# An encoder layer on one core: first MLP product with banks seeded by ScalarE, weight sums on VectorE, functions a step later

## The chip, the cores and the metric

The kernel runs on one core of one Trainium2 chip. The metric is the device time of one execution in microseconds (us). The core has TensorE (PE; PEld is its weight load), VectorE (DVE), ScalarE (ACT), GpSimd (POOL) and SyncE (SP), which here issues nearly all DMAs. A matmul writes to PSUM, eight banks of 128 x 512 fp32; everything else works from SBUF.

## What is computed

One layer of an encoder on 2048 tokens of width 1024: a mixer (two kinds of attention), and then the MLP, which is what matters here:

```python
x = x + gt1 * (mixed @ w_o)
h = rmsnorm(x, g_norm2) * (1.0 + sc2) + sh2
x = x + gt2 * (jnp.square(jax.nn.relu(h @ w1)) @ w2)
```

Here `w1` is 1024 x 4096 and `w2` 4096 x 1024. All values are fp32.

## The kernel before

**Precision.** Each fp32 operand is held as two parts: the high part is ScalarE's cast to fp32r, the low part is VectorE's subtraction of that from the fp32 value (`split`, `operand`). A product takes three matmuls: high x high, high x low, low x high, in this order (`mm3`).

**Seven products for eight.** Both MLP products work on 2 x 2 blocks with seven block products (1 to 7), some of whose operands are sums or differences of blocks. Token blocks of 512 (`tb`) come in two pairs, `mb` 1 (tokens 1024 to 2047) and `mb` 0. For the first product (class `First`, line 1431) a pair `j` of hidden tiles, 2 x 128 rows, takes seven *steps*, one for each block product; a step is 4 blocks of the contraction x 3 = 12 matmuls of 128 x 512. There are 16 pairs, so 112 steps for each `mb`.

- `sums` (1463) makes the four sums of weight tiles of a pair, on GpSimd, as soon as `fetch` is called, nine steps ahead of the pair (1839 to 1840); `load` (13 steps ahead) issues the two DMAs of 512 KB. For the very first pair `fetch` is called in the sixth row of the out-projection (`Mixed`, 1778, by `then`, 1821), for the second pair only when its first operand is prepared.
- The products of a pair run in the order `PRODUCTS` = 1, 6, 5, 7, 2, 3, 4 (1283). Products 1, 6, 5, 7 and 3 take a PSUM bank each; 2 adds onto the bank of 1, 4 onto that of 7. `run` (1475) ends with the reads of the bank: ScalarE copies product 1 to a tile `u`; VectorE adds 6 to it, makes `v` (5 + u), the hidden block c22 (7 + v), c12 (3 + v) and c21 (bank 7 + u); ScalarE makes c11 from bank 1.
- `hidden` (1521) puts relu and square of each block on ScalarE at once, behind the add; `keep` (1528) stores rows for later, and the differences of hidden blocks that the second product needs are made two ticks later (`rest`, `end`).

**Order.** All matmuls and, in this part, all instructions of every queue stand in the order in which the code issues them. The loop at the end of the kernel goes step by step: `prepare` of operands for the steps ahead (eight tiles of the pool `opp`: seven steps ahead in First, three in Second), then the jobs that `at(n, ...)` put at this step, then `run`, then a tick of `later`, a list of jobs that wait a number of ticks. So on every engine an instruction waits for all that stand ahead of it in its queue, and `later.add(1, ...)` means the end of the same step.

**Around it.** Ahead of First of `mb` 1 run the last eight rows of the out-projection (`Mixed`); each row ends in a VectorE add from its bank, and its store to DRAM two ticks later. Among these rows the right-hand operands of `mb` 1 are made by `right_blocks` (1369): load of four rows, a VectorE multiply with the norm's row and a ScalarE shift for each, and then in three jobs (`scale`, `mixed`, `rest`) the high and low parts of seven blocks. During First of `mb` 1, `norm2` (1337) makes the norm rows of token blocks 1 and 0: squares on ScalarE, sums on VectorE, column sums on TensorE (`pvm`), a root in five small GpSimd operations, a diagonal on VectorE (`ndgm`), and a matmul that spreads it (`psr`). VectorE also makes four sums a pair for the second product (`second_sums`, 1531, tiles `w2s`; for `mb` 0 `outer_sums`). Next comes `Second` of `mb` 1 (four products of 16 steps, four banks each), among which `right_blocks` makes the operands of `mb` 0, and `update` (1615) adds results to rows `scr_x`. Then First of `mb` 0, Second for products 1 and 6, and three `Outer` blocks, each a set of seven products on two column blocks, with Second of products 5 and 7 between them.

**Banks.** Four PSUM banks are `zb`, two are `db`, and two are `ab` (the accumulator pair of the attention). `pp` (1301) hands them out in turn, `zb, zb, ab, db, ...`, to all of these. `Outer` already seeds: when product 1 ends, ScalarE copies its bank to a second one, onto which 6, 7 and 4 add; 3 adds onto the bank of 5, and 2 onto that of 1 (`HOME`, 1286).

**Names in the profile.** Every instruction has line 42, the helper that keeps the order, so groups go by tiles: `ps<-h,opw` are the matmuls of First, `ps<-oph,opv` those of Second, `ps<-opr,ol` and `ps_s` those of Outer, `pso` those of the out-projection; `opr<-w` and `opw<-w` or `opw<-ts` are the parts of First's weights (`w` raw, `ts` sums), `cu`, `cv`, `cx`, `cy` the tiles u, v, c22 and c11, `ca`, `cb`, `ce` the differences, `cxr` and `xr` rows of the out-projection, `ty`/`cy` with `h` the right blocks, `txn` the norm's rows, `txu`/`txo` rows of results.

Of the kernel before, what the change touches and what calls it, by code (L numbers as in the profile page):

```python
# [79 lines left out]
def encoder_kernel(ctx, tc, xT, c, g1, g2, w_in, w_rest, gqk, bias, w_o, w1, w2, w_ada, b_ada, out):  # L80
# [1202 lines left out]
    PRODUCTS = (1, 6, 5, 7, 2, 3, 4)  # L1283
# [10 lines left out]
    if True:  # L1294
# [6 lines left out]
        pp = Banks(zb, zb, ab, db, zb, zb, ab, db)  # L1301

# [23 lines left out]
        def bank(nm):  # L1326
            return pp.tile([P, TB], F32, tag="ps", name=f"ps{nm}")
# [9 lines left out]
        def norm2(tb, step):  # L1337
# [14 lines left out]
            def second():  # L1352
                dg = norm_rstd(np2, pp, acc, f"m{tb}")

                def third():
                    pr = bank(f"r{tb}")
# [10 lines left out]
            at(step + 3 * KT + 4, lambda: later.add(2, second))  # L1367

        def right_blocks(mb, k, home):
# [20 lines left out]
            def scale():  # L1390
                for nm, tb, kk in tiles:
                    dve.tensor_tensor(y[nm], y[nm], rows[tb], op=ALU.mult)
                    act.activation(
                        y[nm], y[nm], AF.Identity, scale=aff[:, 1, kk : kk + 1], bias=mod[:, 3 * KT + kk : 3 * KT + kk + 1]
                    )
                high(1, "11")
# [22 lines left out]
            return load, scale, mixed, rest  # L1419
# [11 lines left out]
        class First(Step):  # L1431
# [4 lines left out]
            def __init__(self, mb, j, i):  # L1436
                self.mb, self.j, self.i, self.nm = mb, j, i, f"{mb}_{j}_{i}"
                if mb and j == 0 and i in PRODUCTS[:2]:
                    self.tiles = self.frees = 0

            def prepare(self, home=None):
                if (home is None) != (self.tiles > 0):
                    return
                d, j, i = self.fetch(), self.j, self.i
                src = {1: d["11"], 2: d["12"], 4: d["22"]}.get(i)
                self.w = operand(d["S", i] if src is None else src, f"w{self.nm}", dst=home)

            def load(self):
                d, j = First.pair.setdefault((self.mb, self.j), {}), self.j
                if not d:  # L1450
                    t = raw_pair([P, 2, KT, P], F32, f"w1_{self.mb}_{j}")
                    for s in range(2):
                        d[s] = t[:, s]
                        sp.dma_start(d[s], w1[2 * j + s])
                return d
# [7 lines left out]
            def sums(self, d):  # L1463
                for s in range(2):
                    d[f"{s + 1}1"] = d[s][:, 0:HK, :].rearrange("p k f -> p (k f)")
                    d[f"{s + 1}2"] = d[s][:, HK:KT, :].rearrange("p k f -> p (k f)")
                s1, s2, s4 = (temp(f"s{self.nm}_{n}") for n in (0, 1, 3))
                s3 = d["21"]
                column_sum(pool, s1, d["21"], d["22"], ALU.add)
                column_sum(pool, s2, s1, d["11"], ALU.subtract)  # L1470
                column_sum(pool, s3, d["11"], d["21"], ALU.subtract)
                column_sum(pool, s4, d["12"], s2, ALU.subtract)
                d["S", 5], d["S", 6], d["S", 7], d["S", 3] = s1, s2, s3, s4

            def run(self):
                d, i, nm = First.pair[self.mb, self.j], self.i, self.nm
                home = {2: 1, 4: 7}.get(i, i)
                if home == i:
                    d["ps", i] = bank(nm)
                ps = d["ps", home]  # L1480
                for k in range(HK):
                    ks = slice(k * P, (k + 1) * P)
                    h = hops[i, k]
                    first, last = home == i and k == 0, k == HK - 1
                    mm3(ps, self.w[:, 0, ks], self.w[:, 1, ks], h[:, 0, :], h[:, 1, :], first, last, home != i)
                if i == 1:
                    d["u"] = kept(f"u{nm}")
                    act.copy(d["u"], ps)
                if i == 6:
                    column_sum(dve, d["u"], ps, d["u"], ALU.add)  # L1490
                if i == 5:
                    d["v"] = column_sum(dve, kept(f"v{nm}"), ps, d["u"], ALU.add)
                if i == 7:
                    d["c22"] = self.hidden(column_sum(dve, kept(f"x{nm}"), ps, d["v"], ALU.add), 3)
                if i == 2:
                    d["c11"] = kept(f"y{nm}")
                    act.activation(d["c11"], ps, AF.Relu)
                    act.activation(d["c11"], d["c11"], AF.Square)
                    c11 = d["c11"]
                    later.add(2, lambda: self.keep(1, c11))  # L1500
                if i == 3:
                    c12 = self.hidden(column_sum(dve, d["v"], ps, d["v"], ALU.add))

                    def rest():
                        t1 = column_sum(dve, kept(f"a{nm}"), c12, d["c11"], ALU.subtract)
                        self.keep(5, t1)
                        d["t2"] = column_sum(dve, kept(f"b{nm}"), d["c22"], t1, ALU.subtract)
                        self.keep(6, d["t2"])
                        self.keep(7, column_sum(dve, c12, d["c22"], c12, ALU.subtract))

                    later.add(2, rest)
                if i == 4:
                    c21 = self.hidden(column_sum(dve, d["u"], ps, d["u"], ALU.add), 2)
# [5 lines left out]
                    later.add(2, end)  # L1519
# [95 lines left out]
        def update(mb, r, odd, acc, loads, adds, keep=True):  # L1615
# [354 lines left out]
```

## Time and profile before

| | |
|---|---|
| time, median of 3 runs (lowest to highest) | 2582.78 us (2579.35 to 2585.35) |
| the profiled execution: time, span | 2583.59 us, 2581.9 us |
| mean granted TensorE clock | 0.999 |
| PE busy in First of `mb` 1, Second of `mb` 1, First of `mb` 0, the rest | 311.85 of 320.07, 178.54 of 181.27, 306.21 of 306.91, 403.58 of 405.89 us |
| VectorE busy in the same stretches | 255.40, 136.78, 236.22, 337.86 us |
| waits of TensorE by engine, longest in total: `z` for VectorE `p` (attention) | 7.1 us in 15 |
| `psr` for VectorE `ndgm` | 4.9 us in 2 |
| `ps` for ScalarE `cu` | 2.4 us in 4 |

A row of a timeline gives the start and the length in us, the engine, the operation, output <- inputs, partitions x elements, the number of merged instructions, and in brackets the idle time ahead of it with the engine that ended it. A row of a stage table gives start:end, length, the busy us (and instructions) of PE, PEld, DVE, ACT and POOL, the granted TensorE clock, the DMA share and GB/s. PE's busy time is modelled, so an operand that comes a little late can lie inside it: a stage's length against its number of matmuls says more than its idle time.

### The profile page before, as it was taken

The numbers are of one execution on the slowest core, as the hardware profiler recorded it, in microseconds if no ns is written. First come the engines' busy times: TensorE is split into PE (matmuls) and PEld (weight loads), VectorE is DVE, ScalarE is ACT, GpSimd is POOL, SyncE is SP. The second block draws the span as 40 slices with busy tenths as digits, with TensorE's granted clock in tenths as the row PEclk, the third lists the DMA queues.
The fourth block names the chain that finished last, engine by engine and source line by source line (L and its number), as shares of the span: only waits on it lengthen the run. The fifth ranks groups of instructions, "written<-read, shape, count | busy, mean of one in ns | idle before, by whom it ended". The sixth has DMA issues, their size and how long they took to land. (4 is left out here: it accounts for less than half of the span.)

```text
span 2581.9 us, 39420 instructions
## 1 busy us (share of the span) xinstructions
PE 2546.8 (99%) x12484; PEld 2112.9 (82%) x12484; DVE 2031.6 (79%) x3401; ACT 1448.3 (56%) x2785; POOL 950.4 (37%) x1256
## 2 busy tenths in 40 slices
PE   9999999999999999999999999999999999999999
PEld 7888888888888888887888877887888878888887
DVE  7656767887789879998768787777787886798987
ACT  6333435668866676666744544565444445465655
POOL 4330144777766677677603333200123320000000
PEclk9999999999999999999999999999999999999999
DMA  9879879788887788756787876786577766866773
GB/s 354 330 296 363 336 286 290 215 238 277 272 262 233 234 281 260 240 195 195 226 331 245 290 261 247 261 302 236 212 248 266 250 241 241 315 222 242 266 272 123
DMA packets 276944, 674.80 MB, mean 261 GB/s; under 512 B 29952, under 2 KB 75008, under 8 KB 266112
## 3 DMA queue, kind: packets, MB, share of 16 engines
q1 hardware_dynamic: 275440, 667.57, 74.7%
q10 hardware_dynamic: 1296, 4.72, 0.4%
q8 instruction: 99, 1.62, 0.3%
q14 instruction: 109, 0.89, 0.1%
HBM read 461.93 MB, written 210.24 MB: 260 GB/s over the span
## 5 line engine op out<-in xcount | busy, mean ns | idle before, releaser
L42 PE MATMUL ps<-h,opw 128*128 128x512 f32 x2664 | 609.9, 390 | 4.0 <-ACT cu L42 2.4
L42 PEld LDWEIGHTS ps<-h,opw 128*128 128x128 f32 x2664 | 498.1, 188 | 113.8 <-ACT cu L42 5.7
L42 PE MATMUL ps<-oph,opv 128*128 128x512 f32 x1536 | 353.3, 391 | 2.7 <-ACT opv L42 1.6
L42 POOL TENSOR_TENSOR b<-p 128x512 f32<-128x512 f32 (+1 forms) x320 | 292.5, 914 | 168.1 <-DVE p L42 92.1
L42 ACT CAST wth<-wt 128x512 fp32r<-128x512 f32 (+3 forms) x544 | 257.7, 484 | 172.3 <-PE wt L42 162.3
L42 PEld LDWEIGHTS ps<-oph,opv 128*128 128x128 f32 x1536 | 289.0, 188 | 66.3 <-ACT opv L42 2.7
L42 DVE TENSOR_TENSOR wtl<-wt,wth 128x512 fp32r<-128x512 f32 (+3 forms) x544 | 291.7, 548 | 59.4 <-ACT wth L42 56.9
L42 PE MATMUL pt<-w,ht 128*128 128x512 f32 x1248 | 288.2, 391 | 0.0
L42 POOL TENSOR_TENSOR ts<-w 128x512 f32<-128x512 f32 x32 | 48.5, 1515 | 616.9 <-DMA w<-in_w_dram 516.0
L42 PEld LDWEIGHTS pt<-w,ht 128*128 128x128 f32 x1248 | 233.0, 188 | 47.7
L42 DVE TENSOR_TENSOR_SCAN p<-z,p,zero 128x512 f32<-128x512 f32 x192 | 245.9, 1282 | 25.7 <-ACT z L42 18.3
L42 PE MATMUL acc<-wth,v 128*128 128x512 f32 (+3 forms) x544 | 220.6, 410 | 0.0
L42 ACT ACTIVATE z<-z 128x512 f32<-128x512 f32 (+1 forms) x320 | 166.5, 521 | 55.1 <-PE z L42 49.3
L42 PE MATMUL z<-k,q 128*128 128x512 f32 (+3 forms) x640 | 185.6, 371 | 7.8 <-DVE p L42 7.1
L42 DVE TENSOR_TENSOR opw<-w,opw 128x512 fp32r<-128x512 f32 x127 | 100.8, 796 | 111.5 <-ACT opw L42 111.5
L42 PE MATMUL acc<-wtl,v 128*128 128x512 f32 (+3 forms) x544 | 185.4, 347 | 0.0
L42 POOL TENSOR_TENSOR e<-e,cols 128x640 f32<-128x640 f32 (+4 forms) x128 | 142.9, 1123 | 83.3 <-DVE cols L42 57.1
L42 PE MATMUL wt<-ident,b 128*128 128x128 f32 x1088 | 171.4, 273 | 1.0 <-DVE cols L42 0.3
L42 PEld LDWEIGHTS wt<-ident,b 128*128 128x128 f32 x1088 | 136.3, 140 | 42.2 <-DVE wtl L42 1.9
L42 PE MATMUL po<-fx,ow 128*128 128x512 f32 x576 | 161.7, 393 | 1.0 <-DMA ow<-scr_wo 1.0
L42 DVE TENSOR_TENSOR oph<-hw,oph 128x512 fp32r<-128x512 f32 x128 | 90.4, 706 | 80.0 <-ACT oph L42 80.0
L42 ACT CAST opr<-r 128x512 fp32r<-128x512 f32 x168 | 104.7, 625 | 83.2 <-PE ps L42 46.6
(210 smaller groups left out, 4849.2 us busy)
## 6 DMA issues: line engine op xcount, KB each, us to landing
q<-scr_q SPq DMA_DIRECT2D x128, 256.0 KB, 5.2
w<-in_w_dram SPq DMA_DIRECT2D x64, 512.0 KB, 5.5
hw<-scr_hid SPq DMA_DIRECT2D x64, 512.0 KB, 6.3
k<-scr_k SPq DMA_DIRECT2D x240, 128.0 KB, 4.4
v<-scr_v SPq DMA_DIRECT2D x120, 256.0 KB, 4.1
wa<-in_w_ada_dram SPq DMA_DIRECT2D x48, 512.0 KB, 6.2
ow<-scr_wo SPq DMA_DIRECT2D x24, 1024.0 KB, 5.9
hw<-scr_s SPq DMA_DIRECT2D x48, 512.0 KB, 7.0
```

The source lines that it names most:

```text
L42: return lambda *x, **y: self.tc.keep_in_program_order(f(*x, **y))
```

## The change

- First runs its products in the order 1, 5, 6, 3, 7, 2, 4 and uses the homes of `Outer`: product 1 ends in a ScalarE copy of its bank to another one, from the accumulator pair (`seeded`), onto which 6, 7 and 4 add; 3 adds onto the bank of 5. ScalarE copies products 5 and 6 out of their banks. VectorE makes only c12 (bank 5 + copy of 6) and c22 (bank 6 + copy of 5); ScalarE's relu reads c11 and c21 from the banks. Products 1 and 5, the norm's matmuls and Outer's products 1 and 5 take banks from `fresh`, the other six.
- The square (and the relu of c12 and c22) stands a step later; the differences and the stores behind them stand one to three steps later.
- The four weight sums of a pair are VectorE's, one to a step from nine steps ahead. For the first two pairs of each `mb` all four stand together: pair 0 of `mb` 1 in the sixth row of the out-projection, right behind its load; pair 1 at its eighth, with its load; pair 0 of `mb` 0 six steps ahead, pair 1 two.
- The norm's `second` stands a step later, and `third` six ticks behind it instead of three.
- `right_blocks` for `mb` 0: the multiply stands a step earlier and the casts a step later than the shift, which keeps its place.
- In `update`, rows are stored three ticks behind their add instead of one, and the fourth load and add of product 6 stand two steps later.

```diff
-    PRODUCTS = (1, 6, 5, 7, 2, 3, 4)
+        fresh, seeded = Banks(zb, zb, db), Banks(ab)
...
-                dg = norm_rstd(np2, pp, acc, f"m{tb}")
+                dg = norm_rstd(np2, fresh, acc, f"m{tb}")
...
-                later.add(3, third)
+                later.add(6, third)
...
-            at(step + 3 * KT + 4, lambda: later.add(2, second))
+            at(step + 3 * KT + 4, lambda: later.add(3, second))
...
-            def fetch(self):
+            def fetch(self, m=None):
                 d = self.load()
-                if "11" not in d:
-                    self.sums(d)
+                for n in range(4) if m is None else (m,):
+                    pr, a, b, op = ((5, "21", "22", ALU.add), (6, 5, "11", ALU.subtract), (3, "12", 6, ALU.subtract), (7, "11", "21", ALU.subtract))[n]
+                    d[pr] = column_sum(dve, d["21"] if pr == 7 else temp(f"s{self.nm}_{pr}"), d[a], d[b], op)
                 return d
...
                 if i == 1:
-                    d["u"] = kept(f"u{nm}")
-                    act.copy(d["u"], ps)
-                if i == 6:
-                    column_sum(dve, d["u"], ps, d["u"], ALU.add)
-                if i == 5:
-                    d["v"] = column_sum(dve, kept(f"v{nm}"), ps, d["u"], ALU.add)
+                    d["ps", 6] = bank(f"{nm}_s", seeded)
+                    act.copy(d["ps", 6], ps)
+                if i in (5, 6):
+                    d["p", i] = kept(f"p{nm}")
+                    act.copy(d["p", i], ps)
+                if i == 3:
+                    d["c12"] = self.hidden(column_sum(dve, d["p", 6], ps, d["p", 6], ALU.add))
                 if i == 7:
-                    d["c22"] = self.hidden(column_sum(dve, kept(f"x{nm}"), ps, d["v"], ALU.add), 3)
+                    d["c22"] = self.hidden(column_sum(dve, d["p", 5], ps, d["p", 5], ALU.add), 3)
...
-            def hidden(self, c, i=None):
-                act.activation(c, c, AF.Relu)
-                act.activation(c, c, AF.Square)
-                if i:
-                    later.add(2, lambda: self.keep(i, c))
+            def hidden(self, c, i=None, src=None):
+                if src is not None:
+                    act.activation(c, src, AF.Relu)
+
+                def square():
+                    if src is None:
+                        act.activation(c, c, AF.Relu)
+                    act.activation(c, c, AF.Square)
+                    if i:
+                        later.add(2, lambda: self.keep(i, c))
+
+                later.add(2, square)
                 return c
...
-                    later.add(1, lambda: sp.dma_start(scr_x[2 * mb + odd, HK * r + n], x))
+                    later.add(3, lambda: sp.dma_start(scr_x[2 * mb + odd, HK * r + n], x))
...
-                update(mb, 0, 1, "s", spread(0, 1, 2, 6), spread(4, 5, 6, 10))
+                update(mb, 0, 1, "s", spread(0, 1, 2, 8), spread(4, 5, 6, 12))
...
-                        Outer.banks[pr, n] = bank(f"{self.nm}_{n}")
+                        Outer.banks[pr, n] = bank(f"{self.nm}_{n}", fresh)
...
-                    Outer.banks[6, n] = bank(f"{self.nm}_s{n}")
+                    Outer.banks[6, n] = bank(f"{self.nm}_s{n}", seeded)
...
-            steps += [First(mb, j, i) for j in range(NP) for i in PRODUCTS]
+            steps += [First(mb, j, i) for j in range(NP) for i in OUTER]
...
-                    at(begin + 7 * j - 9, f.fetch)
+                    for m in range(4):
+                        at(begin + 7 * j - 9 + (m if j > 1 else 0), lambda f=f, m=m: f.fetch(m))
             if mb:
+                at(begin - 1, steps[begin + 7].fetch)
...
-                    for n, job in zip((0, 5, 7, 9), right_blocks(0, k, temp)):
-                        at(begins + n, job)
+                    pieces = right_blocks(0, k, temp)
+                    for n, m in ((0, 0), (4, 4), (5, 5), (6, 6), (7, 2), (9, 3)):
+                        at(begins + n, pieces[m])
...
             else:
                 at(begin - 8, steps[begin].load)
+                at(begin - 6, steps[begin].fetch)
```

More of the change, by code (lines that the diff above doesn't have):

```diff
@@ L1324, in kept, with bank @@
             return accp.tile([P, TB], F32, tag="c", name=f"c{nm}")
-        def bank(nm):
-            return pp.tile([P, TB], F32, tag="ps", name=f"ps{nm}")
+        def bank(nm, banks=pp):
+            return banks.tile([P, TB], F32, tag="ps", name=f"ps{nm}")
         steps, jobs = [], {}
@@ L1395, in scale, with begin @@
                     )
+            def scale():
+                multiply()
+                shift()
+                begin()
+            def begin():
                 high(1, "11")
@@ L1417, in rest @@
                 low(4, "21")
-            return load, scale, mixed, rest
+            return load, scale, mixed, rest, multiply, shift, begin
         class Step:
```

61 lines of the change are left out of this document (25 added, 36 removed).

## The prediction

> **What bounds the kernel now.** I read the page's first part, then busy time by stage, then TensorE's own timeline, and then, for every wait on it, the engine named there. A step is twelve 128x512 matmuls; a pair of the first product is seven steps.
>
> ```profile
> PE 2546.8 (99%) x12484; PEld 2112.9 (82%) x12484; DVE 2031.6 (79%) x3401; ACT 1448.3 (56%) x2785; POOL 950.4 (37%) x1256
> 1365.86:1685.93 320.07, 311.85 (x1378) 254.70 (x1376) 255.40 (x341) 153.59 (x273) 103.46 (x73) 1.00 0.74 263
> 1685.93:1867.20 181.27, 178.54 (x769) 144.86 (x768) 136.78 (x214) 102.19 (x180) 10.56 (x7) 0.99 0.69 252
> 1867.20:2174.11 306.91, 306.21 (x1346) 251.65 (x1344) 236.22 (x312) 143.06 (x252) 89.96 (x58) 1.00 0.69 240
> ```
>
> The stage rows (start:end, length, busy us of PE, PEld, DVE, ACT, POOL, clock) are First for tokens 1024-2047 (mb 1), its Second, and First for mb 0. Both Firsts hold 16x7x12 = 1344 product matmuls, yet the earlier takes 13.2 us more. TensorE is the bound nearly everywhere, so a gain can only be a gap of TensorE that closes. Its timeline (start, length, instructions, wait before the row):
>
> ```profile
> 1365.86 5.60 PE L42 MATMUL ps<-h,opr 128*128 128x512 f32 x24
> 1498.51 0.95 PE L42 MATMUL pvm<-ones,r 128*128 128x1 f32 x8
> 1510.56 1.13 PE L42 MATMUL psr<-ndgm,ones 128*128 128x128 f32 x8 [2.78 <-DVE ndgm L42]
> 1599.66 1.16 PE L42 MATMUL psr<-ndgm,ones 128*128 128x128 f32 x8 [2.17 <-DVE ndgm L42]
> 1771.08 16.51 PE L42 MATMUL ps<-oph,opv 128*128 128x512 f32 x61 [1.59 <-ACT opv L42]
> 2069.64 104.63 PE L42 MATMUL ps<-h,opw 128*128 128x512 f32 x456 [0.70 <-ACT cu L42]
> 2174.11 87.20 PE L42 MATMUL ps<-oph,opv 128*128 128x512 f32 x384
> 2261.15 21.92 PE L42 MATMUL ps<-opr,ol 128*128 128x512 f32 x96
> ```
>
> The clean pace is read off the last two rows: 87.04 us for 384 matmuls, 0.2267 each, 2.72 a step, 19.04 a pair. At that pace 1344 matmuls are 304.7 and 768 are 174.1. So mb 0's First loses 2.2 us; mb 1's loses 320.07 - 304.7 less 2 x (0.95 + 1.13) = 4.2 for the norm's own matmuls, 11.2; its Second loses 181.27 - 174.1 = 7.2. **The most that can be won is 20.6 us.**
>
> Why First loses: VectorE cannot keep the pace.
>
> ```profile
> 1518.31 0.68 DVE L42 TENSOR_TENSOR opw<-w,opw 128x512 fp32r<-128x512 f32 x1
> 1518.91 0.69 DVE L42 TENSOR_TENSOR w2s<-w2s 128x512 f32<-128x512 f32 x1
> 1519.51 0.69 DVE L42 TENSOR_TENSOR cx<-ps,cv 128x512 f32<-128x512 f32 x1
> 1520.23 1.30 ACT L42 ACTIVATE cx<-cx 128x512 f32<-128x512 f32 x2 [4.19 <-DVE cx L42]
> 1521.42 1.29 POOL L42 TENSOR_TENSOR ts<-w 128x512 f32<-128x512 f32 x1 [11.73 <-DMA w<-in_w_dram]
> 1522.07 1.19 DVE L42 TENSOR_TENSOR opw<-w,opw 128x512 fp32r<-128x512 f32 x1 [1.88 <-ACT opw L42]
> 1523.19 1.78 DVE L42 TENSOR_TENSOR w2s<-w2s 128x512 f32<-128x512 f32 x1
> 1973.16 0.69 DVE L42 TENSOR_TENSOR cu<-ps,cu 128x512 f32<-128x512 f32 x1
> 2050.66 0.69 DVE L42 TENSOR_TENSOR cu<-ps,cu 128x512 f32<-128x512 f32 x1
> ```
>
> Two things cost it time. An operation on two SBUF tiles follows the last by 0.60 us alone (0.69 long), but lasts up to 1.78 while GpSimd runs one of the four weight sums. And after each VectorE add, ScalarE's relu and square (1.30) stand ahead of its next cast, so VectorE's next operand subtraction waits 1.88. The last two rows are one job four pairs apart: 77.50 us, 19.38 a pair against TensorE's 19.04. The lag grows until TensorE waits (2069.64); while the norm adds work it grows faster.
>
> **The change, part by part.**
>
> *Weight sums to VectorE, banks seeded by ScalarE.* A pair loses three VectorE adds out of PSUM and gains four sums: with 7 subtractions, 2 adds, 4 differences and 4 sums for the second product it has 21 operations, 12.6 us at 0.60, about 15 with the norm's adds and the chained ones, of 19.04. GpSimd's collisions go. ScalarE gains two copies of 0.59 (row 1870.12 below), 1.2 us a pair, beside its 153.59 busy us of 320: free. Relu and square move a step behind, so the 1.88 waits go too. What could be late instead: the seed must be in its bank when product 6 starts, two steps after product 1.
>
> ```profile
> 1870.12 0.59 ACT L42 COPY cu<-ps 128x512 f32<-128x512 f32 x1 [1.58 <-PE ps L42]
> 1851.47 1.30 POOL L42 TENSOR_TENSOR ts<-w 128x512 f32<-128x512 f32 x1 [198.11 <-DMA w<-in_w_dram]
> ```
>
> Today's copy of product 1 in the same place waits only for TensorE and takes 0.59; the step between gives it 2.72. The tightest new turn is product 4: it now waits for the add that reads bank 6 after product 7, one step between instead of two, so that add may lag 2.72 - 0.69 = 2.0 us. With 15 of 19 us used I expect it on time. mb 0's first sums, six steps ahead of 1867.20, at about 1851, meet weights that have landed by 1851.47: nothing.
>
> The hidden rows' stores stand one to three steps later; at seven `c` tiles a pair, twelve tiles last 12 steps or more, and none is kept ten: nothing.
>
> *Norm.* The waits of 2.78 and 2.17 end a chain from the column matmul (1498.51) to the diagonal; in it GpSimd's root stands behind weight sums:
>
> ```profile
> 1504.51 1.74 POOL L42 TENSOR_TENSOR ts<-w,ts 128x512 f32<-128x512 f32 x1
> 1507.54 1.02 POOL L42 TENSOR_TENSOR nym<-nvm,mhalf 128x4 f32<-128x4 f32 x1 [1.30 <-DVE nvm L42]
> 1509.72 0.69 DVE L42 TENSOR_TENSOR ndgm<-ident,nym 128x512 f32<-128x512 f32 x1 [2.26 <-POOL nym L42]
> ```
>
> The chain ran from 1498.51 to 1510.4, 11.9 us; the new distance of six steps gives 16.3, and GpSimd has nothing else to do. Both waits go. Together I take 10.2 of the 11.2 us and 1.7 of the 2.2.
>
> *Second of mb 1.* At 1771.08 TensorE waits for casts that stand behind a burst on ScalarE (x4 and x3 are the merged instructions):
>
> ```profile
> 1765.49 2.95 ACT L42 ACTIVATE ty<-ty,mod,aff 128x512 f32<-128x512 f32 x4 [1.52 <-DVE ty L42]
> 1768.34 1.65 ACT L42 CAST h<-ty 128x512 fp32r<-128x512 f32 x3
> 1769.89 0.61 ACT L42 CAST oph<-hw 128x512 fp32r<-128x512 f32 x1
> 1772.00:1776.00 4.00, 4.00 (x11) 3.17 (x12) 4.00 (x7) 0.69 (x2) 0.00 (x0) 0.57 0.94 367
> 1510.00:1515.00 5.00, 4.44 (x24) 3.88 (x25) 4.96 (x9) 3.32 (x7) 0.00 (x0) 1.00 0.39 149
> ```
>
> The change puts multiply, shift and casts in three steps, so 4.6 us become 2.95 and 1.65; and the rows' stores, which block SyncE's queue until VectorE is through, stand two steps later, with the fourth load and add moved by two steps since its tile comes free later: nothing by itself, four steps still lie between them. After the wait the granted clock fell to 0.57 for 4 us: 11 matmuls instead of 17.6, another 1.5 us. Of the 7.2 I take 4.5, between 0 (other waits take their place) and 7.2, nearest to what the two rows explain, 1.59 + 1.5, with the smaller waits of the same kind.
>
> *The opening of First.* Here something new is late. The sums of pair 0 now stand in VectorE's queue at the sixth out-projection row, right behind the issue of their weights:
>
> ```profile
> 1355.17 0.86 SPq L42 DMA_DIRECT2D w<-in_w_dram  x2
> 1359.32 0.75 DVE L42 SCALAR_TENSOR_TENSOR cxr<-pso,mod,cxr 128x512 f32<-128x512 f32 x1
> 1359.98 0.68 DVE L42 TENSOR_TENSOR h<-cy,h 128x512 fp32r<-128x512 f32 x1
> 1363.19 1.82 POOL L42 TENSOR_TENSOR ts<-w 128x512 f32<-128x512 f32 x1 [59.17 <-ACT h L42]
> 1363.77 0.74 DVE L42 SCALAR_TENSOR_TENSOR cxr<-pso,mod,cxr 128x512 f32<-128x512 f32 x1
> 1364.43 1.12 DVE L42 TENSOR_TENSOR opr<-w,opr 128x512 fp32r<-128x512 f32 x1
> 1370.16 1.81 POOL L42 TENSOR_TENSOR ts<-w 128x512 f32<-128x512 f32 x1 [0.50 <-DMA w<-in_w_dram]
> ```
>
> GpSimd had stood idle and began at 1363.19, so the weights landed about then. VectorE will wait from 1359.3 to 1363.2, do four sums (2.6, to 1365.8), the row's add that ran at 1359.32 (0.7), the 3.8 us of work between 1359.98 and 1363.77, the next row (0.7), and only at 1371.0 the first operand's low part, there at 1371.6 instead of 1365.5. ScalarE's high part follows the same work and comes at about 1370.2. TensorE, which began at 1365.86, then does two matmuls, waits for the low part, and ends its first step at 1374.0 instead of 1368.6: **5.4 us lost**. Behind it are queued the row stores in SyncE's queue and pair 1's weights, issued a step earlier in the code but, behind those stores, some 2 us later: they land at 1372.2 (now 1370.16); VectorE gets to their sums at about 1372.2, and the third step's low part is done at 1376.3, when TensorE reaches that step at 1376.7. Bounds: 3.5 if the weights land 2 us earlier, 7 if the third step is late too.
>
> *Banks.* Both banks of the accumulator pair now hold product 6 of Outer, and the following Second takes one of them as its third bank, 6 matmuls (1.36 us) after it starts.
>
> ```profile
> 2337.37 4.92 PE L42 MATMUL ps<-oph,opv 128*128 128x512 f32 x21
> 2339.09 1.41 DVE L42 SCALAR_TENSOR_TENSOR txo<-ps_s,mod,txo 128x512 f32<-128x512 f32 x2 [0.90 <-DMA txo<-scr_x]
> ```
>
> It needs the bank at 2338.73; the first of the two reads ends at 2339.84: 1.1 us, 1.2 with the release. Second of product 7 meets the same turn after the next Outer, and I take the same for it: 2.4, between 0.4 (without the 0.90 for the DMA) and 3.
>
> **Sum** against the profiled execution's 2583.59 us (span 2581.9, 1.7 around it; 0.8 over the median, 2582.78): -10.2 - 1.7 - 4.5 + 5.4 + 2.4 = -8.6, so 2575.0.
>
> **Rivals.**
> *The clock falls at the opening.* The gap there is about 4.4 us, longer than any in these stages; 1.59 was followed by a clock of 0.57, 2.78 was not (row 1510.00). If it falls, 1.5 us more, 2576.5. The Trainium skill, "TensorE: Matmul & The Clock Gate", Part 1, says that an idle window of about 3.4 us, free-running, halves the clock for about as long. By that rule the dip is likely here and would cost some 1.7 us, an estimate from the page's figures; the trace agrees in size with the 0.57 row, but shows that the length of the wait alone does not decide.
> *Second keeps its loss.* VectorE's order there still waits for ScalarE block by block, and loads still queue behind stores. Then 4.5 is not won: 2579.5.
> *Slower: VectorE stays the bound.* If its waits (weights not landed for the sums, ScalarE's casts behind more copies) add 4.4 us to the 15 of a pair, product 4 waits in every pair, since the lag it tolerates falls to 2.0 us. First of mb 1 then keeps its 11.2, mb 0 pays 16 x (19.38 - 19.04) = 5.4 instead of 2.2, Second inherits the lag: 2583.6 + 5.4 + 2.4 + 3.2 = 2594.6. For it: VectorE was 255.40 of 320.07 us busy; against it: the rows of 1.78 and 1.88, whose causes both go.
> *The opening is covered* (weights land before VectorE needs them): 2569.6.
>
> **How the numbers follow.** Forecast 0.45, clock 0.15, Second's loss kept 0.20, VectorE the bound 0.15, opening covered 0.05. About 0.2% (5.2 us) is what a measurement of this kernel can tell from no change, so faster means below 2577.6: most of the forecast and the clock case and all of the last, 0.55; same 0.30; slower 0.15. The range runs from the covered opening with Second's whole 7.2 won, 2567, to Second's loss kept with the opening at 7, the clock down and the banks at 3, near 2583, and 3 more for the spread of runs: 2567 to 2586.
>
> **What would show it.** Right: no wait for ndgm; the row psr without a bracket; First of mb 1 near 310 plus the opening, mb 0 near 305; a gap of some 5 us before the first matmuls of First, VectorE waiting there for w; a wait of about 1 us at the third bank of Second of mb 0, for products 5 and 7; VectorE's two-tile operations all near 0.69 in First. Wrong: waits for cx or ps in every pair, or First of mb 1 above 320. The forecast falls if the opening loses much more than 7 us, or if Second's waits come back under other names.

## The result, and the profile after

| | before | after |
|---|---|---|
| median (lowest to highest), 6 runs each | 2584.07 us (2578.88 to 2586.21) | 2573.09 us (2569.26 to 2576.96) |
| the profiled execution: time, span | 2583.59, 2581.9 us | 2573.75, 2572.0 us |

The ratio is 0.996, with a 95% interval of 0.9945 to 0.9975: the kernel became about 11 us faster. The forecast was 2575.0. The span fell by 9.9 us, against a forecast sum of 8.6.

The page's busy times and then the stages of the profile after, with the same columns as in the prediction: First of `mb` 1, its Second, First of `mb` 0, and most of the rest.

```profile
PE 2542.0 (99%) x12484; PEld 2115.9 (82%) x12484; DVE 1965.5 (76%) x3433; ACT 1483.7 (58%) x2849; POOL 747.3 (29%) x1128
```
```profile
1366.00:1681.87 315.87, 311.89 (x1378) 257.83 (x1377) 227.16 (x363) 174.53 (x309) 3.62 (x10) 0.99 0.79 270
1681.87:1856.20 174.33, 174.33 (x770) 144.10 (x769) 136.35 (x220) 101.43 (x179) 0.00 (x0) 1.00 0.72 258
1856.20:2160.80 304.60, 304.60 (x1346) 252.22 (x1344) 203.47 (x321) 162.12 (x285) 0.00 (x0) 1.00 0.72 243
```

VectorE has more instructions in First of `mb` 1 (363 for 341) and is busy for less time (227.16 for 255.40 us). Second of `mb` 1 and First of `mb` 0 now take, within 0.2 us, what their matmuls take at the clean pace, 174.1 and 304.7. First of `mb` 1 does not yet: 315.87. TensorE's waits from 1300 us on (in total, times, longest) say where the remainder lies:

```profile
PE ps L42 <- ACT opr L42: 3.7, 1, 3.7
PE ps L42 <- DVE txo L42: 2.9, 2, 1.8
PE po L42 <- DMA ow<-scr_wo: 0.5, 1, 0.5
PE ps L42 <- DVE opr L42: 0.2, 1, 0.2
```

`cu`, `cx`, `ndgm`, `opv` and `oph` are gone from this list. What is left is the opening of First (`opr`) and the third bank of Second (`txo`), the two waits that the change itself brought.

**The opening**, in the timeline of the profile after: VectorE's sums, the row's add behind them, the first operand's high part (ScalarE) and low part (VectorE), and TensorE. The two windows below have the granted clock third from the end of the row.

```profile
1362.85 0.69 DVE L42 TENSOR_TENSOR ts<-w 128x512 f32<-128x512 f32 x1 [2.94 <-DMA w<-in_w_dram]
...
1364.91 0.68 DVE L42 TENSOR_TENSOR w<-w 128x512 f32<-128x512 f32 x1
...
1369.22 0.61 ACT L42 CAST opr<-w 128x512 fp32r<-128x512 f32 x1
1369.89 1.22 PE L42 MATMUL ps<-h,opr 128*128 128x512 f32 x2 [3.73 <-ACT opr L42]
1370.62 0.68 DVE L42 TENSOR_TENSOR opr<-w,opr 128x512 fp32r<-128x512 f32 x1
1371.35 7.67 PE L42 MATMUL ps<-h,opr 128*128 128x512 f32 x22 [0.24 <-DVE opr L42]
1378.87 2.88 PE L42 MATMUL ps_s<-h,opw 128*128 128x512 f32 x12
```
```profile
1368.00:1372.00 4.00, 1.87 (x4) 1.06 (x5) 3.92 (x8) 3.41 (x8) 0.00 (x0) 0.71 0.78 295
1372.00:1376.00 4.00, 4.00 (x11) 3.12 (x10) 3.93 (x7) 2.52 (x5) 0.00 (x0) 0.50 0.06 22
```

VectorE waits 2.94 us for the weights, and the low part is there at 1371.30; the prediction had said 1371.6. The first matmuls come 3.73 us late; the two of them and their wait cost another 1.0; then the clock stands at 0.50, and 22 matmuls take 7.52 us (1371.35 to 1378.87) where 22 x 0.2267 are 4.99, 2.5 more. Together that is 7.2 us.

**The norm** needs no bracket on `psr` any more. Its chain in the profile after, and behind it three rows of the profile before:

```profile
1506.71 0.95 PE L42 MATMUL pvm<-ones,r 128*128 128x1 f32 x8
1507.72 0.15 DVE L42 TENSOR_SCALAR nvm<-pvm 128x4 f32<-128x4 f32 x1
1508.01 1.01 POOL L42 TENSOR_TENSOR nym<-nvm,mhalf 128x4 f32<-128x4 f32 x1 [203.31 <-DVE nvm L42]
1510.18 0.69 DVE L42 TENSOR_TENSOR ndgm<-ident,nym 128x512 f32<-128x512 f32 x1 [2.31 <-POOL nym L42]
...
1523.99 1.06 PE L42 MATMUL psr<-ndgm,ones 128*128 128x128 f32 x8
```
```profile
1507.31 0.15 DVE L42 TENSOR_SCALAR nvm<-pvm 128x4 f32<-128x4 f32 x1
...
1596.51 0.15 DVE L42 TENSOR_SCALAR nvm<-pvm 128x4 f32<-128x4 f32 x1
1596.74 1.02 POOL L42 TENSOR_TENSOR nym<-nvm,mhalf 128x4 f32<-128x4 f32 x1 [7.04 <-DVE nvm L42]
```

From the column matmul to the diagonal's end it takes 4.2 us (11.9 before), and the spreading matmul runs 13 us after that. The time is won at VectorE's read of the column sums (`nvm`): it begins 1.0 us after the start of the column matmul; in the profile before it began 8.8 us after it (1507.31 against 1498.51). GpSimd was not what was late: it stood idle for 1.30 and 7.04 us until the two reads of `nvm` had come.

**VectorE's two-tile operations** are at one length again. The groups of the sums for the second product between 1400 and 1500 us (busy us, mean ns of one), after and before:

```profile
L42 DVE TENSOR_TENSOR w2s<-w2s 128x512 f32<-128x512 f32 x23 | 15.7, 684 | 0.0
```
```profile
L42 DVE TENSOR_TENSOR w2s<-w2s 128x512 f32<-128x512 f32 x20 | 20.3, 1014 | 0.0
```

**The banks**, in TensorE's timeline after: six matmuls, then a wait for the third bank, in Second for products 5 and 7.

```profile
2324.01 1.52 PE L42 MATMUL ps<-oph,opv 128*128 128x512 f32 x6
2326.62 42.50 PE L42 MATMUL ps<-oph,opv 128*128 128x512 f32 x186 [1.08 <-DVE txo L42]
...
2448.45 11.86 PE L42 MATMUL ps<-oph,opv 128*128 128x512 f32 x51 [1.77 <-DVE txo L42]
```

### The profile page after: what moved, and what is told of

It reads as the page before. It is cut to its first block, busy times and chain, and to the rows that moved or that the text cites. A ratio compares the mean times of both kernels' runs of the same rounds, so it can differ in the third digit from the quotient of the medians.

```text
span 2572.0 us, 39296 instructions
## 1 busy us (share of the span) xinstructions
PE 2542.0 (99%) x12484; PEld 2115.9 (82%) x12484; DVE 1965.5 (76%) x3433; ACT 1483.7 (58%) x2849; POOL 747.3 (29%) x1128
## 4 chain that ended last, share of the span: by engine, by line
PE 85%; DVE 6%; DMA 3%; ACT 2%; issue 2%; POOL 1%; SPq 1%; DVEq 0%; POOLq 0%; ACTq 0%
PE ps L42 30%; PE ps_s L42 12%; PE pt L42 11%; PE acc L42 6%; PE wt L42 6%; PE po L42 4%; PE pf L42 4%; PE z L42 4%; PE pq L42 3%; PE cz L42 2%; DVE p L42 2%; PE pso L42 1%; DVE opr L42 1%; DMA txo<-scr_x 1%; PE ct L42 1%
## 5 line engine op out<-in xcount | busy, mean ns | idle before, releaser
L42 PE MATMUL ps<-h,opw 128*128 128x512 f32 x1512 | 358.6, 389 | 0.0
L42 PEld LDWEIGHTS ps<-h,opw 128*128 128x128 f32 x1512 | 283.6, 188 | 58.9
L42 PE MATMUL ps_s<-h,opw 128*128 128x512 f32 x1152 | 277.0, 389 | 0.0
L42 PEld LDWEIGHTS ps_s<-h,opw 128*128 128x128 f32 x1152 | 216.1, 188 | 44.9
L42 DVE TENSOR_TENSOR opw<-w,opw 128x512 fp32r<-128x512 f32 x127 | 87.3, 691 | 95.0 <-ACT opw L42 95.0
```

The source lines that it names most:

```text
L42: return lambda *x, **y: self.tc.keep_in_program_order(f(*x, **y))
```

## The experiments

The theory is the forecast's: First waited because VectorE collided with GpSimd and stood behind ScalarE's relu and square; the opening is late because VectorE's queue stands at weights that haven't landed; the third bank waits for Outer's read; Second of `mb` 1 gains from the split of the right blocks and the later stores. All edits are made to the kernel after the change. The table gives the median, the ratio to the kernel before on the same chip with its 95% interval, and from each profile the lengths of: First of `mb` 1 with the opening, Second of `mb` 1, First of `mb` 0, and the rest to the end of the span. First of `mb` 1 is counted from the end of the out-projection, 27.2 us after the start of its last 120 matmuls: that end falls anywhere from 1363.6 to 1367.1 us in these executions, and all of that difference arises ahead of 1324 us, where no edit reaches.

| kernel | median | ratio (95%) | First 1 | Second 1 | First 0 | rest |
|---|---|---|---|---|---|---|
| before | 2584.07 | 1 | 320.1 | 181.3 | 306.9 | 407.8 |
| after | 2573.09 | 0.996 (0.9945 to 0.9975) | 315.9 | 174.3 | 304.6 | 411.2 |
| e1 sums on GpSimd | 2571.00 | 0.9947 (0.9934 to 0.9959) | 314.5 | 174.1 | 304.7 | 412.4 |
| e4 relu at once | 2571.41 | 0.9945 (0.9928 to 0.9961) | 314.2 | 174.1 | 304.6 | 409.8 |
| e9 both | 2599.92 | 1.0057 (1.004 to 1.0074) | 326.4 | 175.1 | 318.7 | 410.6 |
| e5 norm near | 2573.71 | 0.9953 (0.9938 to 0.9968) | 316.2 | 174.9 | 304.6 | 410.5 |
| e2 opening late | 2572.23 | 0.9951 (0.9939 to 0.9964) | 316.0 | 175.5 | 304.6 | 410.5 |
| e3 banks | 2569.89 | 0.9939 (0.9926 to 0.9951) | 315.8 | 175.4 | 304.6 | 407.8 |
| e8 e2 and e3 | 2567.81 | 0.9934 (0.992 to 0.9947) | 315.2 | 175.1 | 304.6 | 407.7 |
| e10 e8, seed first | 2564.25 | 0.9917 (0.9902 to 0.9932) | 309.8 | 175.5 | 304.6 | 407.9 |
| e6 blocks back | 2576.38 | 0.9966 (0.9957 to 0.9976) | 315.9 | 178.5 | 304.6 | 410.4 |
| e7 stores back | 2575.04 | 0.9961 (0.9944 to 0.9978) | 312.2 | 177.2 | 304.6 | 410.6 |
| e11 both back | 2578.54 | 0.9976 (0.9967 to 0.9985) | 314.7 | 180.4 | 304.6 | 410.7 |

Only e9 and e10 have an interval that lies clear of the one after. What the others show is read from the lengths of the stages and from the waits, in one profile of each.

### First: the sums' engine and the deferred functions, a square of four

**e1_gpsimd** gives the sums back to GpSimd, and leaves all else.

```diff
-                    d[pr] = column_sum(dve, d["21"] if pr == 7 else temp(f"s{self.nm}_{pr}"), d[a], d[b], op)
+                    d[pr] = column_sum(pool, d["21"] if pr == 7 else temp(f"s{self.nm}_{pr}"), d[a], d[b], op)
```

> The changed kernel with one thing undone: all weight sums of First are GpSimd's again, at their new places. Theory (VectorE was too slow for two causes, collisions with GpSimd and relus ahead of casts, and either one gone is enough; the opening loss is VectorE waiting for weights): no wait at the opening, First of mb 1 near 308.5 us instead of 315.9, First of mb 0 near 304.6, in all 7.4 us less than the changed kernel, about 2565.7 or 0.993 of before, though VectorE operations of 1.78 us are back. Rival (the collisions were what made VectorE too slow): First of mb 0 at 306.5 or more with waits that grow, First of mb 1 315 or more, in all 2573 or more.

First of `mb` 0 stays at 304.7, so the collisions alone don't make TensorE wait there, as long as relu and square stand a step later. In First of `mb` 1, where the norm's adds come on top, one wait of 1.17 us for VectorE's add comes back (at 1443.04). The gain expected at the opening was missed, 314.5 for 308.5 us and 2571.00 for 2565.7, because the opening only changes its form: the wait of 3.7 us for `opr` is gone, but there is one of 2.19 us for the seed, because ScalarE's copy to the second bank stands behind a cast that needs the second pair's sums:

```profile
1370.77 0.62 ACT L42 CAST opw<-ts 128x512 fp32r<-128x512 f32 x1 [0.67 <-POOL ts L42]
1371.41 0.57 ACT L42 COPY ps_s<-ps 128x512 f32<-128x512 f32 x1
...
1372.03 4.56 PE L42 MATMUL ps_s<-h,opw 128*128 128x512 f32 x12 [2.19 <-ACT ps_s L42]
```

**e4_relu_now** makes relu and square at once again, with the sums on VectorE.

```diff
-                later.add(2, square)
+                square()
```

> The changed kernel with relu and square at once behind the add again. Theory (collisions and relu waits each cost VectorE some 4 to 5 us a pair, and either one gone is enough): two waits of 1.9 us a pair come back, VectorE needs about 18.8 us of 19.04 a pair without the norm, so First of mb 0 stays near 304.6 to 305.5; in First of mb 1 the norm's adds push it over, 1 to 3 us longer than 315.9; in all 2573 to 2576. Rival (the deferral is what did it): waits of TensorE in every pair of both Firsts, First of mb 0 at 307 or more, in all 2577 or more.

First of `mb` 0 is 304.6 here too: with no collisions, VectorE has room for the waits behind ScalarE. First of `mb` 1, expected 1 to 3 us longer, is not longer either (314.2 for 315.9), and no wait for VectorE's adds stands in it. Either half of the cure is enough, but for the one wait of e1.

**e9_gpsimd_relu** is both edits together, so of First's change only the new order, the seeded banks and the later places of the sums, differences and stores are left.

> Weight sums on GpSimd as in e1, and relu and square at once as before the change: what is left of the change is the seeding, the order of the products, the distances and the stores. Theory (both causes are back, VectorE needs about 18.5 us a pair without and 20 with the norm's adds): waits grow in First of mb 1, which is 4 us or more longer than e1's 314.5, and First of mb 0 lies above 305; in all 2575 or more. Rival (the seeding, which takes three adds from VectorE, is enough by itself): Firsts as in e1, in all 2571.

This is 27 us slower than after, and slower than before the change. TensorE's waits in the two Firsts, and five rows of the timeline:

```profile
PE ps_s L42 <- DVE cp L42: 21.0, 25, 2.6
```
```profile
1440.73 1.77 DVE L42 TENSOR_TENSOR w2s<-w2s 128x512 f32<-128x512 f32 x1
1442.43 1.75 DVE L42 TENSOR_TENSOR r<-r,txn 128x512 f32<-128x512 f32 x1
1443.60 1.72 POOL L42 TENSOR_TENSOR w<-w 128x512 f32<-128x512 f32 x1
1444.10 0.68 DVE L42 TENSOR_TENSOR cp<-ps_s,cp 128x512 f32<-128x512 f32 x1
1444.84 3.02 PE L42 MATMUL ps_s<-h,opw 128*128 128x512 f32 x12 [2.06 <-DVE cp L42]
```

Two collided operations (1.77 and 1.75) stand ahead of the add that reads bank 6 after product 7, and product 4, which adds onto that bank, waits 2.06 us for it. That is the mechanism of the prediction's slower rival at its place. Its price was higher: First of `mb` 0 loses 318.7 - 304.7 = 14.0 us, where the rival had put 5.4.

**e5_norm_near** brings `third` and `second` of the norm back to their old distances.

```diff
-                later.add(6, third)
+                later.add(3, third)
...
-            at(step + 3 * KT + 4, lambda: later.add(3, second))
+            at(step + 3 * KT + 4, lambda: later.add(2, second))
```

> The changed kernel with the norm's old distances: second after two ticks, third three steps later. Theory (the norm's chain was late because GpSimd and VectorE were, and takes 4.2 us now from the column matmul to the diagonal): three steps are 8.2 us, no wait for ndgm, the same time as the changed kernel, 2573. Rival (the distance was needed): a wait of 1 us or more at each of the two psr, 2575 or more.

No wait for `ndgm` comes back, and the median is that of the kernel after. The chain of 4.2 us fits in the old three steps (8.2 us), so the longer distance bought nothing. The free GpSimd wasn't what shortened the chain either: in e1, with the sums back on GpSimd, it takes 5.2 and 4.1 us (from 1503.02 to 1508.18 and from 1586.52 to 1590.61), and VectorE reads `nvm` there 1.0 us after the start of the column matmul, both times. What shortened it is that VectorE no longer lags at this place.

### The opening and the banks

**e2_open_late** puts the sums of the first two pairs of `mb` 1 at the first operand that needs them; the loads stay.

```diff
+                if i == 5 and 5 not in d:
+                    self.fetch()
...
-                steps[n + LEFT].load() if n + LEFT < KT else steps[KT].fetch() if n + LEFT == KT else None
+                steps[n + LEFT].load() if n + LEFT < KT else steps[KT].load() if n + LEFT == KT else None
...
-                at(begin - 1, steps[begin + 7].fetch)
+                at(begin - 1, steps[begin + 7].load)
```

> The changed kernel, but for the first two pairs of mb 1 only the load keeps its place, and the four sums, still VectorE's, stand at the first operand that needs one. Theory (the opening is lost to the place in VectorE's queue, not to the engine): TensorE goes from the out-projection to First without the 3.7 us wait and without the fall of the clock, First of mb 1 near 308.5, in all 2565.7, 0.993 of before. Rival (VectorE has no room there for eight more sums): a wait of 3 us or more comes a few steps later, 2569 or more.

The first matmul stands at 1363.91 with no wait, 6 us earlier than after; 2.1 of these are the out-projection's, which ended earlier in this execution. The rest is lost again at once, at the seed, in a wait of 4.30 us and the fall of the clock behind it, so that First takes 316.0 us as after (315.9):

```profile
1372.39 1.34 ACT L42 CAST opw<-ts 128x512 fp32r<-128x512 f32 x2 [3.29 <-issue]
1373.75 0.57 ACT L42 COPY ps_s<-ps 128x512 f32<-128x512 f32 x1
...
1374.38 5.38 PE L42 MATMUL ps_s<-h,opw 128*128 128x512 f32 x12 [4.30 <-ACT ps_s L42]
```

`prepare` runs ahead of `run`, so the casts of the second pair's operands stand ahead of the seed's copy in ScalarE's queue. They wait for the second pair's sums, and these stand in VectorE's queue behind the low parts of the first pair:

```profile
1369.22 2.49 DVE L42 TENSOR_TENSOR opw<-w,opw 128x512 fp32r<-128x512 f32 x4
1371.63 0.68 DVE L42 TENSOR_TENSOR ts<-w 128x512 f32<-128x512 f32 x1
```

No idle time stands ahead of that sum, so it did not wait for its weights: they were issued from 1359.58 to 1360.46, and no load of weights in this stretch took more than 7.0 us to land. The expected 2565.7 was missed, and the rival, that VectorE has no room here for eight more sums, came true with its wait and its time. The opening was not cured by moving the sums: the next late thing took over.

**e3_banks** keeps the accumulator pair out of the products that follow an Outer: product 1 and 5 of Outer and Second of products 5 and 7 take their banks from `zb, zb, db, db`.

```diff
+        halved = Banks(zb, zb, db, db)
...
-                    Second.banks[i] = [bank(f"{self.nm}_{n}") for n in range(HK)]
+                    Second.banks[i] = [bank(f"{self.nm}_{n}", pp if mb or i in (1, 6) else halved) for n in range(HK)]
...
-                        Outer.banks[pr, n] = bank(f"{self.nm}_{n}", fresh)
+                        Outer.banks[pr, n] = bank(f"{self.nm}_{n}", halved)
```

> The changed kernel, but Outer's products 1 and 5 and the two Seconds between the Outers take their banks in turn from two of the first pool and two of the second, so that no Second needs a bank that still holds product 6. Theory (those two waits for txo are the bank alone): both go, 2.9 us less, 2570.2, 0.9946 of before. Rival (the late reads of the banks hold up something else as soon as this wait is gone): the same time as the changed kernel, 2573.

Both waits for `txo` are gone and the rest is 407.8 us long, as before the change: the banks cost 411.2 - 407.8 = 3.4 us. In all nine profiles that keep the change's banks the rest is 2.0 to 4.6 us longer than 407.8, 2.9 in the mean.

**e8_open_banks** is e2 and e3 together.

> Both of the last two edits. If the losses are separate: 10.3 us less than the changed kernel, 2562.8, 0.992 of before, and no wait of TensorE of more than 0.5 us behind the first out-projection rows. If one hides the other: 2565 or more.

The median is 2567.81: the banks' gain is there, and the wait at the seed stays (3.6 us), so the expectation was missed at the opening by as much as in e2.

**e10_seed_first** is e8, and at the first step of First the second pair's operands are not yet prepared, so that the seed's copy stands ahead of their casts.

```diff
-            while nxt is not None and ready - used + nxt.tiles <= 8:
+            while nxt is not None and ready - used + nxt.tiles <= 8 and not (n == KT and nxt is steps[KT + 8]):
```

> The kernel of e8 with one more edit: at the first step of First of mb 1 no operand beyond pair 0 and the first of pair 1 is prepared, so that no cast that needs pair 1's sums stands ahead of the seed copy in ScalarE's queue. Theory (e2 and e8 waited for the seed copy behind those casts, 4.3 and 3.6 us, and lost the clock after it): the wait goes, First of mb 1 lies near 309 us instead of 315.2, in all 2561 to 2562, 0.991 of before. Rival (weights or VectorE are late at the opening whatever the order): another wait of 2 us or more in the first ten steps, 2565 or more.

In ScalarE's timeline of e10 the copy now runs first, and the casts wait behind it; the second fence has TensorE's waits from 1320 us to the end:

```profile
1368.75 0.57 ACT L42 COPY ps_s<-ps 128x512 f32<-128x512 f32 x1
1371.96 1.35 ACT L42 CAST opw<-ts 128x512 fp32r<-128x512 f32 x2 [2.65 <-DVE ts L42]
```
```profile
PE ps L42 <- ACT cp L42: 1.1, 1, 1.1
PE ps L42 <- DVE oph L42: 0.2, 1, 0.2
```

First of `mb` 1 with its opening takes 309.8 us, so the opening costs about 1 us, the one wait that is left. At 2564.25 us, 2 us above what was expected, this is the fastest kernel of the study, 0.9917 (0.9902 to 0.9932) of before; its span is 2581.9 - 2562.3 = 19.6 us shorter, of which 1.4 lie ahead of First (the out-projection ended earlier), so that 18.2 of the 20.6 that could be won are won.

### Second of mb 1

**e6_blocks_back** undoes the split of the right blocks into multiply, shift and casts at three steps. **e7_stores_back** undoes the later stores and the moved fourth load and add of `update`. **e11_blocks_stores** undoes both.

```diff
-                    for n, m in ((0, 0), (4, 4), (5, 5), (6, 6), (7, 2), (9, 3)):
+                    for n, m in ((0, 0), (5, 1), (7, 2), (9, 3)):
```
```diff
-                    later.add(3, lambda: sp.dma_start(scr_x[2 * mb + odd, HK * r + n], x))
+                    later.add(1, lambda: sp.dma_start(scr_x[2 * mb + odd, HK * r + n], x))
...
-                update(mb, 0, 1, "s", spread(0, 1, 2, 8), spread(4, 5, 6, 12))
+                update(mb, 0, 1, "s", spread(0, 1, 2, 6), spread(4, 5, 6, 10))
```

> The changed kernel with the jobs of the right blocks of mb 0 where they were: multiply, shift and casts in one job. Theory (Second of mb 1 lost 7 us to ScalarE's bursts of 4.6 us, and to loads queued behind stores): waits for opv or oph come back there, Second of mb 1 3 us or more longer than 174.3, in all 2576 or more. Rival (Second only inherited First's lag of VectorE, which is gone): 174 to 175, in all 2573.

> The changed kernel with the rows stored one tick behind their add and the fourth load where it was. Theory (the stores block SyncE's queue ahead of loads that Second needs): waits after loads of hidden rows, Second of mb 1 1 to 3 us longer than 174.3, in all 2574 to 2576. Rival (the place of the stores does not matter once the bursts are split): 174 to 175, in all 2573.

> Both of the last two undone, so that Second of mb 1 has its old order behind the new First. Theory (the order in Second is the cause): 178 to 181, as before the change (181.3), in all 2577 to 2580. Rival (First's lag was the cause): 174 to 175, in all 2573.

Second of `mb` 1 takes 178.5, 177.2 and 180.4 us, where the nine kernels that leave it as the change has it (after, e1 to e5, e8 to e10) lie between 174.1 and 175.5. So with either half undone a loss of 4.2 or 2.9 us is back, and without both it is nearly what it was before, 181.3. Of the 7.0 us won here, 6.1 belong to these two edits. The lengths and times are those expected. A wait for `opv` or `oph` stands in all three again; but idle time tells less than half of it: in e11 it is 2.4 us of 6.3. Three of five stretches of 4 us, first after, then e11:

```profile
1763.00:1767.00 4.00, 4.00 (x19) 3.32 (x18) 3.46 (x6) 2.33 (x5) 0.00 (x0) 1.00 0.68 272
1767.00:1771.00 4.00, 4.00 (x20) 3.30 (x19) 4.00 (x8) 1.62 (x3) 0.00 (x0) 1.00 0.73 240
1779.00:1783.00 4.00, 4.00 (x20) 3.30 (x19) 4.00 (x8) 2.35 (x4) 0.00 (x0) 1.00 0.86 264
```
```profile
1763.00:1767.00 4.00, 2.69 (x11) 1.80 (x11) 3.08 (x6) 2.44 (x5) 0.00 (x0) 1.00 0.93 316
1767.00:1771.00 4.00, 3.57 (x16) 2.63 (x14) 2.79 (x6) 2.16 (x4) 0.00 (x0) 1.00 0.98 389
1779.00:1783.00 4.00, 3.70 (x15) 2.53 (x14) 4.00 (x8) 2.50 (x5) 0.00 (x0) 1.00 0.81 305
```

In the last row TensorE is busy 3.70 of 4 us at full clock and yet shows 15 matmuls where it shows 20 after the change (both counts take in those that only reach into the stretch). Five fewer are 1.1 us at the clean pace, and only 0.3 of it is idle: some matmuls come a little late, and the busy time hides it. The split of the work between the two edits was only seen in one profile of each; all three lengths lie above the spread of the others, e7's by 1.7 us. That the earlier stores cost it by holding SyncE's queue fits that queue's own waits for VectorE's rows (`txu`), 37.3 us in all in e7 and 16.3 after in this stage, but it is not shown by itself, and the moved load and add of e7 were not undone apart from the stores.

e7's profile shows one thing more. Its opening is the change's own, unedited, yet First takes only 312.2 us with it:

```profile
1359.10 0.69 DVE L42 TENSOR_TENSOR ts<-w 128x512 f32<-128x512 f32 x1 [1.97 <-DMA w<-in_w_dram]
...
1366.14 0.74 PE L42 MATMUL ps<-h,opr 128*128 128x512 f32 x2 [2.43 <-ACT opr L42]
1367.60 5.28 PE L42 MATMUL ps<-h,opr 128*128 128x512 f32 x22 [0.73 <-DVE opr L42]
```

In this execution VectorE got the weights 3.75 us earlier than after, but the out-projection ended 2.4 us earlier too, so against TensorE they came 1.3 us earlier. The wait is 2.43 us for 3.73, the 22 matmuls run at full pace, and the opening costs 3.3 us instead of 7.0 (312.2 and 315.9 less 308.9, the matmuls at the clean pace with the norm's). In the seven profiles that keep this opening (after, e3 to e7, e11) its price is between 3.3 and 7.3 us. So it varies from execution to execution, and a good part of that is whether the clock falls; e7's profiled time is the lowest of its five (2569.86 of 2569.86 to 2579.08).

## Why the prediction was right, and where its sizes were off

| step of the prediction | forecast | measured in the profiles |
|---|---|---|
| First of `mb` 1, its own losses | -10.2 | -11.2 |
| First of `mb` 0 | -1.7 | -2.3 |
| Second of `mb` 1 | -4.5 | -7.0 |
| the opening | +5.4 | +7.0 |
| the banks | +2.4 | +3.4 |
| sum | -8.6 | -10.1 (spans: -9.9) |

*The bound.* That the gain could only be closed gaps of TensorE held: the three stages moved toward their matmuls at the clean pace, and none got below it.

*Weight sums, functions, seeds.* All 11.2 us of the first First went: with its opening nearly cured (e10) it takes 309.8, of which 1.07 are the wait that is left, and 304.7 and the norm's 4.2 are 308.9. In the new order the mechanism is shown from both sides. The lag of VectorE comes from the collisions together with the queue behind relu and square; taking away either is enough but for 1.2 us, and leaving both costs 14 us in one First. The tolerance of product 4, "one step between instead of two", is where it shows. What the prediction didn't see is that its two cures were each enough alone. No run has the cures in the old order of products, so what they would be worth without the seeded banks is not shown.

*Norm.* Both waits went, as forecast, but for neither of the two reasons given. The distance of six steps wasn't needed (e5). And GpSimd's root did not stand behind weight sums: the prediction's own row of it has GpSimd idle for 1.30 us until VectorE's `nvm`, and at the second norm it was idle for 7.04. What was late was VectorE's read in its own queue, 8.8 and 8.3 us after the start of the column matmul, so these two waits were a part of VectorE's lag and went with it.

*Second of mb 1.* The term was mis-sized: it took what the rows of waits and the lowered clock explained, 4.5, and counted the rest as doubtful. The rest went too, all 7.0 us; e11 brings 6.1 of them back, mostly hidden inside busy TensorE rows. The reading of the clock's row, 11 matmuls instead of 17.6, sets a count that takes in matmuls at the edges against a count that doesn't; half speed for about 3.4 us is 1.7 us, close to the 1.5 taken. The rival by which Second keeps its loss fell with that.

*The opening.* The chain came out nearly to the row: low part at 1371.30 for 1371.6, wait of 3.7 for the first matmul. The rival beside it, the falling clock, happened as well; it cost 2.5 us where the 0.57 row had given 1.5. It came in six of the seven profiles with this opening, so its chance of 0.15 was too small. The Trainium skill, "TensorE: Matmul & The Clock Gate", Part 1, has the clock halved after an idle window of about 3.4 us; the clock of 0.50 after 3.73 us of waiting agrees with it here, and the section on the hardware below has the waits that don't. The bounds of 3.5 and 7 nearly cover what the seven profiles show, 3.3 to 7.3; the lower one allowed for weights that land 2 us earlier, and in e7 1.3 us against TensorE was enough for it, because the clock did not fall.

*Banks.* Place and cause were right, and e3 shows the whole price: 3.4 us against the profile after, a little over the upper bound of 3, and 2.9 in the mean of nine profiles. The two waits differ from each other and from execution to execution (1.08 and 1.77 after, 1.86 and 0.60 in e1), where 1.2 was taken for both.

All three gains (by 4.1 us together) and both losses (by 2.6) were put too small. That the sum came within 1.3 us of the span's change, and the median within 1.9 us of the forecast, is in part luck: the errors cancelled.

## What to carry to other kernels

When work is moved to an engine whose queue is kept in order, look at the first time it runs, not only at the steady state: a sum whose load has not landed, or a cast whose sum is not made yet, holds up everything that was issued behind it, and the cure for one such wait (e2) uncovers the next in another queue until the order of issue itself is mended (e10). When a stage is compared between two executions, count it from its own start: here up to 3.5 us between two profiles lay ahead of it. When a change has two cures for one lag, test each without the other and both removed; only the square of four says which part does the work and what the bare change would have cost (e9, slower than before). And read a stage's length against its number of matmuls at a clean pace: operands that come a little late can hide several microseconds in rows that count as busy.

## What the runs showed of the hardware

**The granted clock after a wait.** In the stages read here it fell to 0.50 with each wait of TensorE over 3.3 us (3.35 in e4 up to 4.53 in e5), but also with waits of 1.59 us (before) and of 1.86 and 2.19 (e1). Read in rows of 1 us it stood there for about 3.4 us (before, e1, e4, e11) or 6.8 us (after, e2, e3, e5, e6, e8), in which a row of 4 us can show a mean such as 0.57. It did not fall with 2.17 and 2.78 (before), 2.43 (e7), 1.77 (after), nor with any of the 25 waits of e9, up to 2.6 us. e1 and e9 open First with the same wait of 2.19 us for the seed, and only e1 loses clock behind it:

```profile
1372.81 3.02 PE L42 MATMUL ps_s<-h,opw 128*128 128x512 f32 x12 [2.19 <-ACT ps_s L42]
```

Here, in e9, the twelve matmuls take 3.02 us; in the row of e1 shown above they take 4.56. So a wait below 3.4 us can bring the fall, which the idle window that the Trainium skill gives ("TensorE: Matmul & The Clock Gate", Part 1) doesn't cover by itself, and what decides between 1.5 and 2.8 us stays open. At the opening one fall costs 1.1 us (e4, 22 matmuls in 6.13 us) to 2.9 us (e8, 24 in 8.38), against the clean pace.

**VectorE beside GpSimd.** An operation of VectorE on two SBUF tiles of 128x512 takes 0.69 us alone and up to 1.79 while GpSimd adds two such tiles (mean of the group 1014 ns against 684). An add of a PSUM bank to one tile does not stretch: in the rows of e9 above it takes 0.68 us at 1444.10 while the GpSimd sum of 1443.60 runs until 1445.32, and the longest of all 64 such adds of e9 takes 0.69.
